# One Strassen-type quarter more in every second column block of a SwiGLU gate/up product

## The chip, the cores and the metric

The kernel runs on one core of one Trainium2 chip. The metric is the device time of one execution in microseconds. Before the change three runs gave 1871.19, 1870.19 and 1870.70 us; the median is 1870.7 us.

## The reference

One layer of a streaming encoder, 256 tokens of width 2048 in float32: a half-step SwiGLU feed-forward, a mixer with a state-space part and an attention part, a second half-step SwiGLU feed-forward, and a gated per-layer embedding. The change is in the second feed-forward:

```python
def swiglu(h, w_gate, w_up, w_down):
    return (jax.nn.silu(h @ w_gate) * (h @ w_up)) @ w_down
...
        x = x + 0.5 * swiglu(rms_norm(x, ffn2_norm[i]), ffn2_w_gate[i], ffn2_w_up[i], ffn2_w_down[i])
```

Here h is 256 x 2048, w_gate and w_up are 2048 x 5632, w_down is 5632 x 2048.

## The kernel before

**Tiles.** P is 128 and NB is 512. The 256 tokens are two token tiles (TT = 2), the inner dimension of 2048 is sixteen k tiles of 128 (KD = 16), handled four at a time (a quarter of the inner dimension, four quarters in all), and the 5632 columns are eleven column blocks of 512 (NF = 11), numbered f = 0 to 10. A weight quarter of one matrix, 512 x 512 values or 1 MB, comes by one DMA on the SP queue into a tile `raw`, of which there are three. It is used in two halves of two k tiles each.

**Precision.** Every float32 product is made from three products of a rounded format. `split` (L165 to L171) makes a high part (`whi`) by a cast on ScalarE (ACT, L168) and a low part (`wlo`) by a subtraction on VectorE (DVE, L171), both 128 x 1024 for one half. There are four buffers for `whi` and for `wlo`. The activations are split the same way (`nhi`/`nlo`, or `hhi`/`hlo` for the first two quarters of the second feed-forward). A matmul is 128 x 128 by 128 x 512. One half, for both token tiles, takes 12 of them (`gemm_half`, L292, L293 and L297), so a weight quarter takes 24, and a quarter of gate and up together 48.

**The seven products.** In the second feed-forward, blocks f = 1 to 10 treat the first quarter of gate and up in another way (`gemm_seven`). The activations of that quarter are a 2 x 2 matrix of blocks (two token tiles by two halves), the weights are one too (two halves by gate and up: b11 and b21 the halves of gate, b12 and b22 those of up). The 2 x 2 product is made with seven block products instead of eight, in Winograd's form of Strassen's method. Each block product is six matmuls (L452, L453, L455), so the quarter takes 42 instead of 48. Three of the products (P1, P2, P3) use b11, b21 and b22 as they are. The four others (P4 to P7) use sums of weight blocks t1 = b11 + b12, t2 = t1 + b22, t4 = t2 + b21 and t3 = b12 + b22, made on DVE at L459 (tile `sum`, two buffers) and split into `shi`/`slo` (three buffers). The sums of activation blocks that go with them are made once, in f = 0, by `sum_forms`, and kept.

Written order of the products: P1, P2, P5, P6, P4, P7, P3. After that come the other three quarters of gate (12 matmuls to a half, onto the PSUM banks of P2 and P4), then those of up (onto the banks of P3 and one more, the tile p38). `opened` (L531 to L533) reads P1, P6 and P7 out of PSUM after the seven products, `gated` (L537 to L540) reads P2, P4 and P5 after the gate quarters and applies the SiLU, and L545 and L547 close the block. A transpose on DVE (L203, `turned`) and 16 small DMAs on the SP queue for every two blocks (L216, `hT<-mid`) lay the result out for the down product.

**Order.** The program text is not the order of execution: the framework's planner reorders the instructions of each engine by its own costs, and then each engine runs its list strictly in order, waiting on semaphores. `put_off(n, fn)` hands work to the n-th following `step()`. PSUM has four single banks (`acc`) and two double ones (`aux`). A block uses all six: P1, P2, P4, P5 in `acc`, P6 with P7 and P3 with its neighbour in `aux`.

**Buffers of activations.** `halves("n")` has four tiles. The second feed-forward's input uses two of them (its quarters 2 and 3), and `sum_forms` a third. `com("h")` has two tiles of 128 x 1024.

Of the kernel before, what the change touches and what calls it, by code (L numbers as in the profile page):

```python
# [9 lines left out]
F32 = mybir.dt.float32  # L10
# [6 lines left out]
P = 128  # L17
# [9 lines left out]
NB = 512  # L27
# [6 lines left out]
def layer_kernel(ctx: ExitStack, tc: tile.TileContext, a: dict, shapes: dict, out: bass.AP):  # L34
# [29 lines left out]
    def uid(s):  # L64
        count[0] += 1
        return f"{s}_{count[0]}"
# [98 lines left out]
    def split(hi, lo, src, scale=None, pinned=False):  # L165

        if scale is None:
            copy = nc.scalar.copy(hi, src)  # L168
            if pinned:
                pin(copy)  # L170
            nc.vector.tensor_tensor(out=lo, in0=src, in1=hi.bitcast(F32), op=ALU.subtract)  # L171
        else:
            split_each(hi.unsqueeze(1), lo.unsqueeze(1), src.unsqueeze(1), [scale])
# [104 lines left out]
    def weight_halves(w, k0, nk, n0, own=None):  # L278

        raw = wp.tile([P, 4, NB], F32, tag="raw", name=uid("raw"), bufs=3)  # L280
        src = w[k0 * P : (k0 + nk) * P, n0 : n0 + NB].rearrange("(j p) n -> p j n", p=P)
        nc.sync.dma_start(raw[:, :nk, :], src)
        return weight_split(raw, nk, own)
# [141 lines left out]
        split(*both, sums.rearrange("p (z t) -> p z t", z=4))  # L425
        return both

    def gemm_seven(act, sums, ws, n0, nkt, pool, first, second):

        raws = []  # L430
        for w in ws:
            raw = wp.tile([P, 4, NB], F32, tag="raw", name=uid("raw"), bufs=3)
            nc.sync.dma_start(raw, w[: 4 * P, n0 : n0 + NB].rearrange("(j p) n -> p j n", p=P))
            raws.append(raw)
        b11, b21, b12, b22 = (raw[:, 2 * h : 2 * h + 2, :] for raw in raws for h in range(2))
        parts = act(0)

        def whole(k, t):
            return [[u[:, 2 * k + j, t * P : (t + 1) * P] for j in range(2)] for u in parts]

        def summed(z):
            return [[u[:, z, j * P : (j + 1) * P] for j in range(2)] for u in sums]

        def product(ps, left, src, own, stop):
            hi, lo = (
                (pool if own else wp).tile([P, 2, NB], F32R, tag=s, name=uid(s), bufs=3 if own else None)
                for s in (("shi", "slo") if own else ("whi", "wlo"))
            )
            split(hi, lo, src)
            lh, ll = left  # L450
            for j in range(2):
                nc.tensor.matmul(ps, lhsT=lh[j], rhs=hi[:, j], start=j == 0, stop=False)  # L452
                nc.tensor.matmul(ps, lhsT=ll[j], rhs=hi[:, j], start=False, stop=False)  # L453
            for j in range(2):
                nc.tensor.matmul(ps, lhsT=lh[j], rhs=lo[:, j], start=False, stop=stop and j == 1)  # L455

        def add(x, y):
            t = pool.tile([P, 2, NB], F32, tag="sum", name=uid("sum"), bufs=2)
            nc.vector.tensor_tensor(out=t, in0=x, in1=y, op=ALU.add)  # L459
            return t  # L460

        p1, p2 = acc(), acc()
        product(p1, whole(0, 0), b11, False, True)
        product(p2, whole(1, 0), b21, False, False)
        step()
        t1 = add(b11, b12)
        p5 = acc()
        product(p5, summed(0), t1, True, True)
        t2 = add(t1, b22)
        p67 = aux()  # L470
        product(p67[:, :NB], summed(1), t2, True, True)
        step()
        t4 = add(t2, b21)
        p4 = acc()
        product(p4, whole(1, 1), t4, True, False)
        t3 = add(b12, b22)
        product(p67[:, NB:], summed(2), t3, True, True)
        step()
        p38 = aux()
        product(p38[:, :NB], summed(3), b22, False, False)  # L480
        step()
        put_off(0, first, p1, p67)
        for w, banks, fresh in ((ws[0], [p2, p4], False), (ws[1], [p38[:, :NB], p38[:, NB:]], True)):
            for k0 in range(4, nkt, 4):
                part = act(k0 // 4)
                for half in list(weight_halves(w, k0, 4, n0)):
                    begin = k0 == 4 and half[0] == 0
                    end = k0 + 4 >= nkt and half[0] == 1
# [3 lines left out]
            if not fresh:  # L492
                put_off(0, second, p2, p4, p5)
        return p38

    def ffn(i, xn, nxt, bg=None):
        wg, wu, wd = (a[f"ffn{i}_w_{s}"][0] for s in ("gate", "up", "down"))
# [22 lines left out]
        for f in range(NF):  # L520
            if prep and f == min(early, NF - 1):
                finish(prep)
                side.close()
                prep = None
                hp = pools.enter_context(phase(f"h{i}b"))
            if sevens and f:
                sg, hh = com("sg"), com("h")
                gate_cols, up_cols = ([u[:, t * NB : (t + 1) * NB] for t in range(TT)] for u in (sg, hh))

                def opened(p1, p67, g=gate_cols, u=up_cols):  # L530
                    nc.scalar.copy(g[0], p1)  # L531
                    nc.vector.tensor_tensor(out=u[0], in0=p67[:, :NB], in1=g[0], op=ALU.add)
                    nc.vector.tensor_tensor(out=u[1], in0=p67[:, NB:], in1=u[0], op=ALU.add)  # L533

                def gated(p2, p4, p5, g=gate_cols, u=up_cols, hh=hh):
                    for z, (ps, other) in enumerate(((p2, g[0]), (p4, u[1]))):
# [3 lines left out]
                    nc.vector.tensor_tensor(  # L540
                        out=v, in0=p5.unsqueeze(1).to_broadcast([P, TT, NB]), in1=v, op=ALU.subtract
                    )

                p38 = gemm_seven(xn, sums, (wg, wu), f * NB, KD, sevens, opened, gated)
                nc.vector.tensor_tensor(out=hh, in0=p38, in1=hh, op=ALU.add)  # L545
                for t in range(TT):
                    nc.vector.scalar_tensor_tensor(  # L547
                        out=up_cols[t], in0=up_cols[t], scalar=xn.rs(t), in1=gate_cols[t], op0=ALU.mult, op1=ALU.mult
                    )
# [1001 lines left out]
```

## Time and profile before

| | before |
|---|---|
| median of three runs | 1870.7 us (1870.19 to 1871.19) |
| the profiled execution, its own time | 1872.24 us |
| its span, first to last instruction | 1870.4 us |
| TensorE (PE) busy | 1859.4 us, 9134 matmuls |
| VectorE (DVE) busy | 1310.4 us, 70% |
| ScalarE (ACT) busy | 996.5 us, 53% |
| granted TensorE clock | 1.0 throughout |

PE is the matrix engine and PEld its weight loads, which overlap the matmuls; SPq is the queue that issues DMAs. A line of a timeline has the start, the duration, the engine, the source line, the operation and its tiles, and in brackets how long the engine was idle before and what ended the wait. The seven-product blocks f = 1 to 10 lie between 1097.5 and 1523.3 us of the span; "block" below means one f.

### The profile page before, as it was taken

What the parts mean: (1) busy time and instruction counts of PE and PEld (TensorE: products, weight loads), DVE (VectorE), ACT (ScalarE), POOL (GpSimd) and SP (SyncE); (2) the same over time, 40 slices, a digit from 0 to 9 for tenths busy, and PEclk for the clock granted to TensorE, in tenths of its full rate; (3) what the DMA queues carried; (4) which work ended last, traced back from release to release, by engine and by line L of the source; (5) the groups of instructions that cost most, each with busy time, mean ns of one, the idle gap of its engine ahead of it and who ended that gap; (6) DMA issues with size and microseconds to landing.
All of it is one profiled execution on the core that took longest, in us unless ns stands there. A gap on an engine that the chain in (4) does not pass through costs nothing.

```text
span 1870.4 us, 23938 instructions
## 1 busy us (share of the span) xinstructions
PE 1859.4 (99%) x9134; PEld 1536.3 (82%) x9134; DVE 1310.4 (70%) x1527; ACT 996.5 (53%) x1151; POOL 50.4 (3%) x84
## 2 busy tenths in 40 slices
PE   9999999999999999999999999999999999999998
PEld 7888888888888888878888888888888888888887
DVE  8867665455576776687567678778787866777655
ACT  7444444444456665456695555445454555666554
POOL 0011000000000000010020000000000000000000
PEclk9999999999999999999999999999999999999999
DMA  8788867766655666675645666575666675656563
GB/s 323 242 278 268 267 208 222 231 217 200 217 196 199 212 199 244 185 248 163 222 147 189 218 205 221 203 220 186 203 205 208 225 228 203 204 202 212 189 224 124
DMA packets 230387, 400.06 MB, mean 214 GB/s; under 512 B 26401, under 2 KB 50337, under 8 KB 229985
## 3 DMA queue, kind: packets, MB, share of 16 engines
q1 hardware_dynamic: 227824, 392.81, 63.7%
q0 software_dynamic: 1728, 4.33, 0.7%
q8 instruction: 71, 1.16, 0.3%
q10 hardware_dynamic: 720, 1.41, 0.2%
q14 instruction: 44, 0.35, 0.1%
HBM read 369.26 MB, written 9.83 MB: 203 GB/s over the span
## 4 chain that ended last, share of the span: by engine, by line
PE 92%; ACT 3%; DVE 2%; DMA 1%; SPq 1%; issue 1%; POOL 0%; DVEq 0%; ACTq 0%; POOLq 0%
PE acc L292 26%; PE acc L297 26%; PE acc L293 26%; PE aux L293 3%; PE aux L292 3%; PE aux L297 3%; ACT whi L168 1%; SPq L1061 1%; PE acc L455 1%; DMA raw<-in_w_in 1%; PE aux L452 1%; PE acc L452 1%; PE acc L453 1%; PE aux L455 1%; PE aux L453 1%
## 5 line engine op out<-in xcount | busy, mean ns | idle before, releaser
L171 DVE TENSOR_TENSOR wlo<-raw,whi 128x1024 fp32r<-128x1024 f32 x656 | 798.2, 1224 | 458.9 <-ACT whi L168 455.3
L168 ACT CAST whi<-raw 128x1024 fp32r<-128x1024 f32 x656 | 686.2, 1053 | 758.7 <-PE acc L293 607.9
L292 PE MATMUL acc<-whi,nhi 128*128 128x512 f32 x1408 | 551.0, 391 | 1.2 <-ACT whi L260 0.5
L293 PE MATMUL acc<-whi,nlo 128*128 128x512 f32 x1408 | 548.2, 389 | 0.0
L297 PE MATMUL acc<-wlo,nhi 128*128 128x512 f32 x1408 | 384.4, 389 | 0.0
L292 PE MATMUL acc<-whi,hhi 128*128 128x512 f32 x816 | 317.6, 389 | 0.0
L293 PE MATMUL acc<-whi,hlo 128*128 128x512 f32 x816 | 317.5, 389 | 0.0
L292 PEld LDWEIGHTS acc<-whi,nhi 128*128 128x128 f32 x1408 | 264.3, 188 | 58.3 <-ACT whi L168 1.7
L297 PEld LDWEIGHTS acc<-wlo,nhi 128*128 128x128 f32 x1408 | 264.2, 188 | 55.6 <-DVE wlo L171 0.4
L293 PEld LDWEIGHTS acc<-whi,nlo 128*128 128x128 f32 x1408 | 264.4, 188 | 54.0
L297 PE MATMUL acc<-wlo,hhi 128*128 128x512 f32 x816 | 221.0, 389 | 0.0
L297 PEld LDWEIGHTS acc<-wlo,hhi 128*128 128x128 f32 x816 | 152.8, 188 | 32.5 <-DVE wlo L171 0.9
L293 PEld LDWEIGHTS acc<-whi,hlo 128*128 128x128 f32 x816 | 153.2, 188 | 32.0
L292 PEld LDWEIGHTS acc<-whi,hhi 128*128 128x128 f32 x816 | 153.1, 188 | 31.8
L171 DVE TENSOR_TENSOR hlo<-hT,hhi 128x1024 fp32r<-128x1024 f32 x88 | 107.1, 1218 | 0.0
L168 ACT CAST hhi<-hT 128x1024 fp32r<-128x1024 f32 x88 | 91.8, 1044 | 0.5 <-PE acc L455 0.4
L292 PE MATMUL aux<-whi,nhi 128*128 128x512 f32 x160 | 62.2, 389 | 0.0
L293 PE MATMUL aux<-whi,nlo 128*128 128x512 f32 x160 | 62.2, 389 | 0.0
L297 PE MATMUL aux<-wlo,nhi 128*128 128x512 f32 x160 | 49.3, 389 | 0.0
L171 DVE TENSOR_TENSOR slo<-sum,shi 128x1024 fp32r<-128x1024 f32 x40 | 48.6, 1214 | 0.4 <-ACT shi L168 0.2
L168 ACT CAST shi<-sum 128x1024 fp32r<-128x1024 f32 x40 | 42.1, 1052 | 11.5 <-DVE sum L459 11.4
L297 PEld LDWEIGHTS aux<-wlo,nhi 128*128 128x128 f32 x160 | 30.0, 188 | 6.2
(312 smaller groups left out, 1314.5 us busy)
## 6 DMA issues: line engine op xcount, KB each, us to landing
raw<-in_ffn_w_up SPq DMA_DIRECT2D x88, 1024.0 KB, 5.9
raw<-in_ffn_w_down SPq DMA_DIRECT2D x88, 1024.0 KB, 5.0
raw<-in_ffn_w_gate SPq DMA_DIRECT2D x86, 1024.0 KB, 5.4
raw<-in_w_in SPq DMA_DIRECT2D x32, 1024.0 KB, 5.5
raw<-in_w_out SPq DMA_DIRECT2D x16, 1024.0 KB, 5.1
raw<-in_w_ple_gate SPq DMA_DIRECT2D x16, 1024.0 KB, 5.1
hT<-mid SPq DMA_DIRECT2D x160, 64.0 KB, 5.0
h<-mid SPq DMA_DIRECT2D x176, 32.0 KB, 3.4
```

The lines of the kernel that those rows point to most:

```text
L168: copy = nc.scalar.copy(hi, src)
L171: nc.vector.tensor_tensor(out=lo, in0=src, in1=hi.bitcast(F32), op=ALU.subtract)
L292: nc.tensor.matmul(ps[t], lhsT=lh, rhs=hi[:, j, cols], start=start and j == 0, stop=False)
L293: nc.tensor.matmul(ps[t], lhsT=ll, rhs=hi[:, j, cols], start=False, stop=False)
L297: nc.tensor.matmul(ps[t], lhsT=lh, rhs=lo[:, j, cols], start=False, stop=stop and j == 1)
L452: nc.tensor.matmul(ps, lhsT=lh[j], rhs=hi[:, j], start=j == 0, stop=False)
L453: nc.tensor.matmul(ps, lhsT=ll[j], rhs=hi[:, j], start=False, stop=False)
L455: nc.tensor.matmul(ps, lhsT=lh[j], rhs=lo[:, j], start=False, stop=stop and j == 1)
L1061: nc.sync.dma_start(zt[0][p1 : p1 + HC, z], sv[p0 : p0 + HC, r % 2 * 2 + r // 2])
```

## The change

`gemm_seven` becomes a class `Seven` with the same seven products, and blocks with odd f (1, 3, 5, 7, 9) take two quarters through them, the second between the gate quarters and the up quarters: seven products of quarter 0, gate quarters 2 and 3, seven products of quarter 1, up quarters 2 and 3. The banks of the seven products go on accumulating over both. Blocks with even f still take one quarter. In odd blocks `opened` and `gated` both come after the second seven products; in even blocks they stay after the first seven products and after the gate quarters. The written order of the products is now P1, P5, P6, P4, P7, P2, P3, everywhere. `sum_forms` runs for quarters 0 and 1.

```diff
+    class Seven:
...
+        def product(self, z, left, src, own):
             hi, lo = (
-                (pool if own else wp).tile([P, 2, NB], F32R, tag=s, name=uid(s), bufs=3 if own else None)
+                (self.pool if own else wp).tile([P, 2, NB], F32R, tag=s, name=uid(s), bufs=3 if own else None)
                 for s in (("shi", "slo") if own else ("whi", "wlo"))
             )
             split(hi, lo, src)
+            ps = self.bank(z)
+            begin = self.done == 0
+            end = self.done == self.chunks - 1 and z in ((1, 5, 6, 7, 2, 4) if self.closing else (1, 5, 6, 7))
...
+        def chunk(self, kb):
+
+            raws = []
+            for w, n0 in self.ws:
+                raw = wp.tile([P, 4, NB], F32, tag="raw", name=uid("raw"), bufs=3)
+                nc.sync.dma_start(
+                    raw, w[4 * kb * P : 4 * (kb + 1) * P, n0 : n0 + NB].rearrange("(j p) n -> p j n", p=P)
+                )
+                raws.append(raw)
+            b11, b21, b12, b22 = (raw[:, 2 * h : 2 * h + 2, :] for raw in raws for h in range(2))
+            parts, sums = self.act(kb), self.sums(kb)
...
+            self.product(1, whole(0, 0), b11, False)
+            t1 = self.add(b11, b12)
+            self.product(5, summed(0), t1, True)
+            step()
+            t2 = self.add(t1, b22)
+            self.product(6, summed(1), t2, True)
+            t4 = self.add(t2, b21)
+            self.product(4, whole(1, 1), t4, True)
+            step()
+            t3 = self.add(b12, b22)
+            self.product(7, summed(2), t3, True)
+            self.product(2, whole(1, 0), b21, False)
+            step()
+            self.product(3, summed(3), b22, False)
+            step()
+            self.done += 1
+
+        def column(self, side, kbs):
+
+            banks = [self.bank(z) for z in ((2, 4), (3, 8))[side]]
+            w, n0 = self.ws[side]
+            for kb in kbs:
+                part = self.act(kb)
+                for half in list(weight_halves(w, 4 * kb, 4, n0)):
+                    end = kb == self.last and half[0] == 1 and not (side == 0 and self.closing)
                     for t in range(TT):
-                        gemm_half({t: banks[t]}, (part, half), (t,), fresh and t == 1 and begin, end)
+                        begin = (side, t) == (1, 1) and kb == self.chunks and half[0] == 0
+                        gemm_half({t: banks[t]}, (part, half), (t,), begin, end)
                     step()
...
+                chunks = 1 + f % 2
+                s = Seven(xn, lambda kb: sums[kb], ((wg, f * NB), (wu, f * NB)), KD, sevens, chunks, chunks == 2)
+                rest = range(chunks, KD // 4)
+                s.chunk(0)
+                if chunks == 1:
+                    put_off(0, opened, s)
+                s.column(0, rest)
+                if chunks == 2:
+                    s.chunk(1)
+                    put_off(0, opened, s)
+                put_off(0, gated, s)
+                s.column(1, rest)
...
-                sums = sum_forms(xn(0))
+                sums = [sum_forms(xn(kb)) for kb in range(2)]
```

More of the change, by code (lines that the diff above doesn't have):

```diff
@@ L426, in sum_forms, with __init__, bank @@
         return both
[L428 to L444, printed above, removed]
+    class Seven:
+        def __init__(self, act, sums, ws, nkt, pool, chunks, closing=False):
+            self.closing = closing
+            self.act, self.sums, self.ws, self.pool = act, sums, ws, pool
+            self.chunks, self.last = chunks, nkt // 4 - 1
+            self.banks = {}
+            self.done = 0
+        def bank(self, z):
+            if z not in self.banks:
+                if z in (1, 2, 4, 5):
+                    self.banks[z] = acc()
+                else:
+                    double = aux()
+                    for i, zz in enumerate((6, 7) if z in (6, 7) else (3, 8)):
+                        self.banks[zz] = double[:, i * NB : (i + 1) * NB]
+                    self.banks[6.7 if z in (6, 7) else 3.8] = double
+            return self.banks[z]
+        def product(self, z, left, src, own):
             hi, lo = (
-                (pool if own else wp).tile([P, 2, NB], F32R, tag=s, name=uid(s), bufs=3 if own else None)
+                (self.pool if own else wp).tile([P, 2, NB], F32R, tag=s, name=uid(s), bufs=3 if own else None)
                 for s in (("shi", "slo") if own else ("whi", "wlo"))
@@ L454, in product, with add @@
             for j in range(2):
-                nc.tensor.matmul(ps, lhsT=lh[j], rhs=lo[:, j], start=False, stop=stop and j == 1)
-        def add(x, y):
-            t = pool.tile([P, 2, NB], F32, tag="sum", name=uid("sum"), bufs=2)
+                nc.tensor.matmul(ps, lhsT=lh[j], rhs=lo[:, j], start=False, stop=end and j == 1)
+        def add(self, x, y):
+            t = self.pool.tile([P, 2, NB], F32, tag="sum", name=uid("sum"), bufs=2)
             nc.vector.tensor_tensor(out=t, in0=x, in1=y, op=ALU.add)
@@ L477, in gemm_seven, with whole, summed @@
[L477 to L488, printed above, removed]
+        def chunk(self, kb):
[8 more added lines that the diff above has]
+            parts, sums = self.act(kb), self.sums(kb)
+            def whole(k, t):
+                return [[u[:, 2 * k + j, t * P : (t + 1) * P] for j in range(2)] for u in parts]
+            def summed(z):
+                return [[u[:, z, j * P : (j + 1) * P] for j in range(2)] for u in sums]
+            self.product(1, whole(0, 0), b11, False)
[14 more added lines that the diff above has]
+            self.done += 1
@@ L540, in gated @@
                     nc.vector.tensor_tensor(
[L541 removed]
+                        out=v, in0=s.bank(5).unsqueeze(1).to_broadcast([P, TT, NB]), in1=v, op=ALU.subtract
                     )
[L544 to L545 removed]
+                chunks = 1 + f % 2
[10 more added lines that the diff above has]
+                s.column(1, rest)
+                nc.vector.tensor_tensor(out=hh, in0=s.banks[3.8], in1=hh, op=ALU.add)
                 for t in range(TT):
```

32 lines of the change are left out of this document (7 added, 25 removed).

## The prediction, made before the changed kernel was run

> **What bounds the kernel now.** The page comes first: span, busy times, and the chain of waits that ended last.
>
> ```profile
> span 1870.4 us, 23938 instructions
> PE 1859.4 (99%) x9134; PEld 1536.3 (82%) x9134; DVE 1310.4 (70%) x1527; ACT 996.5 (53%) x1151; POOL 50.4 (3%) x84
> PE 92%; ACT 3%; DVE 2%; DMA 1%; SPq 1%; issue 1%; POOL 0%; DVEq 0%; ACTq 0%; POOLq 0%
> ```
>
> TensorE sets the end, so a matmul removed is time saved as long as its operands arrive. For this stage the view by stretches follows, cut at the first matmul of each block f = 1 to 10; columns are length, then busy us and count of PE, weight loads, DVE, ACT, POOL, then granted clock, DMA share, GB/s.
>
> ```profile
> 1097.50:1139.79 42.29, 42.29 (x187) 34.91 (x186) 32.91 (x33) 21.16 (x23) 0.00 (x0) 1.00 0.59 199
> 1139.79:1182.26 42.47, 42.47 (x187) 34.83 (x186) 31.14 (x31) 20.55 (x22) 0.00 (x0) 1.00 0.71 223
> 1182.26:1225.14 42.88, 42.74 (x187) 34.68 (x186) 37.31 (x37) 22.09 (x24) 0.00 (x0) 1.00 0.57 196
> 1225.14:1267.49 42.35, 42.35 (x187) 34.83 (x186) 31.15 (x31) 20.56 (x22) 0.00 (x0) 1.00 0.72 224
> 1267.49:1310.42 42.93, 42.79 (x187) 34.68 (x186) 37.30 (x37) 22.10 (x24) 0.00 (x0) 1.00 0.57 196
> 1310.42:1352.79 42.37, 42.37 (x187) 34.83 (x186) 31.15 (x31) 20.57 (x22) 0.00 (x0) 1.00 0.72 224
> ...
> 1438.07:1480.95 42.88, 42.73 (x187) 34.68 (x186) 37.22 (x37) 22.09 (x24) 0.00 (x0) 1.00 0.57 196
> 1480.95:1523.29 42.34, 42.34 (x187) 34.79 (x186) 31.34 (x31) 20.98 (x23) 0.00 (x0) 1.00 0.76 239
> sum 425.79, PE 425.22 PEld 347.72 DVE 337.88 ACT 212.79 POOL 0.00; mean PE 42.52 PEld 34.77 DVE 33.79 ACT 21.28 POOL 0.00
> ```
>
> A block has 186 matmuls (42 + 144). What they cost undisturbed is read from the timeline of PE over 96 of them, eight halves:
>
> ```profile
> 1160.51 0.39 PE L292 MATMUL acc<-whi,nhi 128*128 128x512 f32 x1
> ...
> 1182.26 0.39 PE L452 MATMUL acc<-whi,hhi 128*128 128x512 f32 x1
> ```
>
> (1182.26 - 1160.51) / 96 = 0.2266 us, so a block needs 42.14. The ten lose 425.79 - 421.4 = 4.4 us, 0.44 on average; even f lose about 0.22, odd f from 3 on about 0.77. Where, the timeline of DVE at f = 3 shows, beside two rows of f = 2:
>
> ```profile
> 1130.94 1.22 DVE L459 TENSOR_TENSOR sum<-raw,raw 128x1024 f32<-128x1024 f32 x1
> 1132.19 1.22 DVE L459 TENSOR_TENSOR sum<-sum,raw 128x1024 f32<-128x1024 f32 x1
> ...
> 1139.01 1.22 DVE L171 TENSOR_TENSOR wlo<-raw,whi 128x1024 fp32r<-128x1024 f32 x1
> ...
> 1178.80 1.22 DVE L459 TENSOR_TENSOR sum<-raw,raw 128x1024 f32<-128x1024 f32 x1
> 1180.05 1.23 DVE L459 TENSOR_TENSOR sum<-sum,raw 128x1024 f32<-128x1024 f32 x1
> ...
> 1183.61 1.22 DVE L545 TENSOR_TENSOR h<-aux,h 128x1024 f32<-128x1024 f32 x1
> 1184.74 1.22 DVE L171 TENSOR_TENSOR slo<-sum,shi 128x1024 fp32r<-128x1024 f32 x1
> 1185.87 1.41 DVE L547 SCALAR_TENSOR_TENSOR h<-h,sm,sg 128x512 f32<-128x512 f32 x2
> 1187.20 1.22 DVE L459 TENSOR_TENSOR sum<-sum,raw 128x1024 f32<-128x1024 f32 x1
> 1188.33 0.71 DVE L203 STREAM_TRANSPOSE mid<-h 128x512 f32<-128x512 f32 x1
> ...
> 1192.93 2.35 DVE L171 TENSOR_TENSOR wlo<-raw,whi 128x1024 fp32r<-128x1024 f32 x2
> 1195.19 0.69 DVE L532 TENSOR_TENSOR h<-aux,sg 128x512 f32<-128x512 f32 x1
> ```
>
> From 1132.19 to 1139.01 stand six operations of 1024 columns start to start: 1.137 us each. At f = 2 the sums begin 8.85 us before PE (1139.79), at f = 3 only 3.46 (1182.26), and there the tail of the block before (L545, twice L547, two transposes, about 3.7 us by these starts) stands between them. The waits name what PE then lacks:
>
> ```profile
> PEld aux L452 <- ACT shi L168: 2.7, 5, 0.6
> PEld acc L452 <- ACT shi L168: 0.9, 4, 0.2
> ```
>
> The reader is to see that the seven products are the one place here where DVE is nearly too slow: 11 operations (seven low parts, four sums), 12.5 us, for 42 matmuls, 9.52 us. It lives on the 32.6 us of plain quarters after them.
>
> **The change part by part.** All differences are on the span, and what lies around it (1872.24 - 1870.4 us in this execution) stays. This execution lies 1.5 us above the median of the runs, 1870.7; the sum is put on that median.
>
> *Matmuls.* Five blocks lose six each: 30 x 0.2266 = **-6.80 us**.
>
> [...]
>
> *The work that replaces them.* Each of the five new sevens has 11 DVE operations where the plain quarter had four: seven more, 8.0 us, and three more casts of about a microsecond on ACT, which is busy 22 of 42.88. It is hidden behind PE only as far as DVE runs ahead: an odd block's 37.3 busy become 45.3 in about 41.5, and the even one's 31.15 of 42.35 must lend the difference. Without that cover all 8.0 would show. I price a new seven as the old ones: 0.44 on average, five times **+2.2 us**, bounds 0.14 (f = 1) and 0.79 (f = 5), that is +0.7 and +4.0.
>
> *The second seven begins early enough, barely.* There are three raw buffers and a seven holds two. The DMA issues:
>
> ```profile
> 1173.52 0.37 SPq L282 DMA_DIRECT2D raw<-in_ffn_w_gate  x1
> 1188.48 2.10 SPq L282 DMA_DIRECT2D raw<-in_ffn_w_gate  x2
> 1195.35 6.23 SPq L282 DMA_DIRECT2D raw<-in_ffn_w_up  x3
> SPq L282 <- DVE sum L459: 130.6, 19, 14.5
> raw<-in_ffn_w_up SPq DMA_DIRECT2D x39, 1024.0 KB, 5.9
> ```
>
> The quarter fetched at 1173.52 sits in the third buffer; its splits are the pair at 1192.93, and at 1195.35 the buffer is free again. In the changed block that issue is the second seven's up quarter: it lands 5.9 us later, at 1201.3. PE ends the first seven at 1225.14 - 144 x 0.2266 = 1192.5 and 48 matmuls later, at 1203.4, wants it. Lead 2.1 us. From landing, nine DVE operations (10.2 us) and a last pair of low-part matmuls (0.45) remain, against 9.52 of PE: 1.1 us of lead are enough, so it holds by a microsecond. Behind SP's waits stand the other weight quarters, and in even blocks the small hT DMAs; the number of deferred steps in a block stays 16, so these stay in the even blocks.
>
> *Even blocks.* They now follow a seven at 10.9 us instead of 32.6. Their lead falls from 8.85 us to two or three. The loss goes from 0.22 towards the odd blocks' 0.77: 0 to +2.75 in five; middle, **+1.4 us**.
>
> *Order of products, `opened` moved.* P2 and P3 need no sum; both now come last, so where PE waits for `shi` the planner can pull two products (2.7 us) forward instead of one, and in odd blocks L532 and L533 leave the first seven. If this mends the odd blocks' excess of 0.55, four times: -2.2. Against it, the gate raw was last read by t4 (1187.20) and is now last read by P2's split, up to three operations (3.4 us) later: the issue at 1188.48 would be at 1191.9, landing at 5.9 more, 1197.8, and with a cast of one microsecond PE, due there at 1192.5 + 24 x 0.2266 = 1197.9, would wait 0.9. I price the outer bound at a third of that, as splits of another quarter can go first: 15 x 0.3 = +4.5. Of a gain of 2.2 and nothing, which the rows show, I take the middle: **-1.1 us**.
>
> *Second `sum_forms`.* One whole sum, four short ones, one split at f = 0:
>
> ```profile
> 1075.40 0.76 DVE L423 TENSOR_TENSOR h<-h 128x256 f32<-128x256 f32 x2
> 1076.08 0.88 DVE L423 TENSOR_TENSOR h<-h,h 128x256 f32<-128x256 f32 x2
> 1079.14 1.22 DVE L171 TENSOR_TENSOR nlo<-h,nhi 128x1024 fp32r<-128x1024 f32 x1
> 1084.29 1.23 DVE L171 TENSOR_TENSOR wlo<-raw,whi 128x1024 fp32r<-128x1024 f32 x1 [1.44 <-ACT whi L168]
> 1087.01 1.23 DVE L171 TENSOR_TENSOR wlo<-raw,whi 128x1024 fp32r<-128x1024 f32 x1 [1.50 <-ACT whi L168]
> ```
>
> About 1.2 + 1.6 + 1.2 = 4.0 us of DVE once; the gaps behind it cover 2.9, the early start before f = 1 the rest: 0, at worst +4.0. It takes the fourth of four `n` tiles, needed next by the block after this feed-forward, when two are long read. PSUM banks change hands 10.9 us before the next block wants them: 0.
>
> Sum: -6.80 + 2.2 + 1.4 - 1.1 + 0 = **-4.3 us**, so 1870.7 - 4.3 = **1866.4 us**. Its own ends: -6.8 + 0.7 + 0 - 2.2 = -8.3 (1862.4) and, with the terms at their upper ends but the outer bound and `sum_forms`, -6.8 + 4.0 + 2.75 + 0 = -0.05 (1870.7).
>
> **The rivals.** *DVE becomes the bound over a pair.* From an odd block's t1 to the end of the next even seven DVE has 9 + 4 + 11 + 4 + 11 = 39 operations (44.3 us), two tails (7.4) and `opened` with `gated` (about 3.6): 55.3. PE has 3 x 9.52 + 96 x 0.2266 = 50.3. With 3.46 us of lead and 0.45 at the end DVE is 2.0 late per pair, where a pair now loses 0.99: five times 1.0 gives -6.8 + 5.0, **1868.9 us**, no change to be told. For it: there is nearly no slack in that stretch; against: it holds at f = 1 less, where the sums have no late start, and tails can be put off.
>
> *The up quarter comes late in even blocks.* `opened` and `gated` (3.6 us) now come right after the second seven; if the planner puts them ahead of the splits that free the third buffer, the lead of 2.1 becomes -1.5. Each us of lead short of 1.1 costs one, so 2.6 in five blocks, without what they lose now (0.22): 5 x 2.4 = 12; with the second sevens at +2.2: -6.8 + 2.2 + 12 = +7.4, **1878.1 us**. It decides from 1.0 us of delay on. For it: SP's waits on L459 show how often the ring of three is the limit; against: the planner put L532 behind the pair at 1192.93.
>
> *The gain is eaten in neither place:* the low end above, 1862.4.
>
> *The change doesn't do what it says:* if the planner left 48 matmuls in a quarter; the text gives 42, so no chance is kept for it.
>
> **How the numbers follow.** This kernel's measurement tells 0.2% (3.7 us) from no change. The forecast's case 0.44, DVE-bound 0.28, late quarter 0.28. The forecast's case reaches into "same" at its upper end, and the DVE-bound case can be a little better than 1867.0, so: faster 0.42, same 0.30, slower 0.28. The likeliest case alone spans 1862.4 to 1870.7; the range takes in the other two: 1862.4 to 1878.1.
>
> **What would show it.** 30 matmuls fewer; odd blocks near 41.3 us (180 x 0.2266 = 40.8 and half a microsecond), even ones 42.4 to 42.9. Right: DVE about 45 busy in odd blocks, PE waiting in tenths. Wrong: PE waiting over a microsecond for `shi` or `slo` at an even block's t4 (DVE-bound), or for a sum behind a raw DMA (late quarter), or any odd block over 42.9.

## The result: slower by 1.15%, and the profile after

Four runs of the changed kernel gave a median of 1891.99 us (1890.32 to 1893.96), against 1870.47 us for the kernel before beside it: ratio 1.0115, interval 1.0097 to 1.0132. That is 21.5 us more, where 4.3 less were forecast. The profiled execution took 1891.26 us.

The page of the changed kernel, in the same order as before:

```profile
span 1889.5 us, 23927 instructions
PE 1862.9 (99%) x9104; PEld 1537.4 (81%) x9104; DVE 1351.1 (72%) x1568; ACT 1012.3 (54%) x1167; POOL 50.3 (3%) x84
PE 93%; DVE 3%; ACT 3%; issue 1%; DMA 0%; POOL 0%; SPq 0%; DVEq 0%; ACTq 0%; POOLq 0%
```

The 30 matmuls are gone (9134 to 9104), yet PE is busy 3.5 us longer: some of the remaining ones took longer. The chain of waits still says PE 93%. It would not lead anyone to the cause. The view by stretches does, cut at the first matmul of each block, columns as in the prediction:

```profile
1095.63:1138.20 42.57, 41.60 (x181) 33.63 (x180) 39.32 (x39) 23.93 (x26) 0.00 (x0) 1.00 0.57 198
1138.20:1180.54 42.34, 42.34 (x187) 34.91 (x186) 32.05 (x32) 20.58 (x22) 0.00 (x0) 1.00 0.72 224
1180.54:1227.85 47.31, 44.35 (x181) 35.64 (x180) 42.57 (x41) 25.14 (x27) 0.00 (x0) 0.93 0.51 178
1227.85:1271.45 43.60, 42.63 (x187) 34.81 (x186) 33.41 (x33) 20.58 (x23) 0.00 (x0) 1.00 0.68 218
1271.45:1317.67 46.22, 43.26 (x182) 34.77 (x180) 42.52 (x41) 25.09 (x27) 0.00 (x0) 0.96 0.52 182
...
sum 446.34, PE 429.65 PEld 348.73 DVE 376.09 ACT 228.16 POOL 0.00; mean PE 42.97 PEld 34.87 DVE 37.61 ACT 22.82 POOL 0.00
```

The ten blocks take 446.34 us instead of 425.79: 20.6 of the 21.5 us lie here. At 0.2266 us a matmul an odd block needs 180 x 0.2266 = 40.79 and an even one 42.14, all ten 414.6; they lose 31.7 us instead of 4.4. The first pair (f = 1, 2) loses 2.0, the pair f = 3 and 4 already 6.5 + 1.5. Two new things stand in the rows of odd f: DVE is busy 42.5 of 46 to 47 us, and the granted clock is under 1. The same view, with the block f = 3 cut before its second seven, and ten microseconds near its start:

```profile
1180.54:1207.30 26.76, 23.80 (x91) 18.74 (x90) 23.23 (x23) 12.38 (x13) 0.00 (x0) 0.87 0.45 157
1207.30:1227.85 20.55, 20.55 (x91) 16.91 (x90) 19.34 (x20) 12.76 (x15) 0.00 (x0) 1.00 0.58 204
1180.00:1190.00 10.00, 7.04 (x24) 5.08 (x23) 9.26 (x10) 4.21 (x4) 0.00 (x0) 0.78 0.15 39
```

Each half of the block has 90 matmuls, 20.39 us. The half with the second seven, on which the forecast had spent its care, loses 0.16. The first seven loses 6.37: 26.76 - 23.80 = 2.96 of PE idle, and 23.80 - 20.39 = 3.41 of matmuls that run slower. The timeline of PE shows both, and the wait of the even block after it:

```profile
1181.90 0.40 PE L460 MATMUL acc<-shi,nhi 128*128 128x512 f32 x1
...
1183.15 0.73 PE L463 MATMUL acc<-slo,nhi 128*128 128x512 f32 x2 [0.15 <-DVE slo L171]
1186.69 0.80 PE L460 MATMUL aux<-shi,nhi 128*128 128x512 f32 x1 [2.81 <-ACT shi L168]
...
1187.71 0.63 PE L460 MATMUL aux<-shi,nhi 128*128 128x512 f32 x1
1188.14 0.63 PE L461 MATMUL aux<-shi,nlo 128*128 128x512 f32 x1
...
1192.67 0.39 PE L460 MATMUL acc<-whi,hhi 128*128 128x512 f32 x1
...
1234.04 0.50 PE L460 MATMUL acc<-shi,hhi 128*128 128x512 f32 x1 [0.97 <-ACT shi L168]
```

P1 and P5 run, then P6 (`aux<-shi`, the first of the double bank) waits 2.81 us for its cast; after that matmuls start 0.43 us apart (1187.71 to 1188.14) instead of 0.2266, until about 1192.5, so for almost six microseconds. P2 (1192.67), which needs no sum, stands behind all of it. The sum that P6 waits for is t2, and the timeline of DVE says where it was; the last row is t1 of the second seven:

```profile
1177.08 1.22 DVE L467 TENSOR_TENSOR sum<-raw,raw 128x1024 f32<-128x1024 f32 x1
1178.66 1.23 DVE L171 TENSOR_TENSOR wlo<-raw,whi 128x1024 fp32r<-128x1024 f32 x1 [0.36 <-ACT whi L168]
1180.74 1.22 DVE L578 TENSOR_TENSOR h<-aux,h 128x1024 f32<-128x1024 f32 x1 [0.86 <-PE aux L297]
1181.88 1.22 DVE L171 TENSOR_TENSOR slo<-sum,shi 128x1024 fp32r<-128x1024 f32 x1
1183.02 1.41 DVE L580 SCALAR_TENSOR_TENSOR h<-h,sm,sg 128x512 f32<-128x512 f32 x2
1184.34 1.22 DVE L467 TENSOR_TENSOR sum<-sum,raw 128x1024 f32<-128x1024 f32 x1
...
1201.16 1.22 DVE L467 TENSOR_TENSOR sum<-raw,raw 128x1024 f32<-128x1024 f32 x1
```

t1 begins 3.46 us before PE's first matmul, as before the change. Then come a split and the tail of the block before (L578, L580); L578 itself waits 0.86 us for PE to finish that block, so DVE is not behind with its work here: its list holds it. t2 begins at 1184.34, 7.3 us after t1. In the kernel before, t2 followed t1 at once and only then came the tail. The second seven's t1 stands 6.1 us ahead of PE (1207.30). The waits of PE over the whole stage repeat the picture:

```profile
PE aux L460 <- ACT shi L168: 11.2, 4, 2.8
PE acc L460 <- ACT shi L168: 3.9, 4, 1.0
```

Four waits of 2.8 at P6 (odd f from 3 on) and four of 1.0 at P4 (even f from 4 on). They sum to 15 us; about as much again is lost in slower matmuls and small gaps.

### The profile page after: what moved, and what is told of

Read it like the earlier page. It is cut to its first block, busy times and chain, and to the rows that moved or that the text cites. A ratio compares the mean times of both kernels' runs of the same rounds, so it can differ in the third digit from the quotient of the medians.

```text
span 1889.5 us, 23927 instructions
## 1 busy us (share of the span) xinstructions
PE 1862.9 (99%) x9104; PEld 1537.4 (81%) x9104; DVE 1351.1 (72%) x1568; ACT 1012.3 (54%) x1167; POOL 50.3 (3%) x84
## 4 chain that ended last, share of the span: by engine, by line
PE 93%; DVE 3%; ACT 3%; issue 1%; DMA 0%; POOL 0%; SPq 0%; DVEq 0%; ACTq 0%; POOLq 0%
PE acc L292 26%; PE acc L297 26%; PE acc L293 26%; PE aux L293 2%; PE aux L292 2%; PE aux L297 2%; PE acc L460 1%; PE aux L460 1%; PE acc L461 1%; PE aux L463 1%; PE aux L461 1%; PE acc L463 1%; ACT shi L168 1%; DVE slo L171 1%; ACT whi L168 1%; DVE h L580 1%
## 5 line engine op out<-in xcount | busy, mean ns | idle before, releaser
L293 PE MATMUL acc<-whi,hlo 128*128 128x512 f32 x776 | 302.3, 390 | 0.0
L292 PE MATMUL acc<-whi,hhi 128*128 128x512 f32 x776 | 302.2, 389 | 0.0
L297 PE MATMUL acc<-wlo,hhi 128*128 128x512 f32 x776 | 209.1, 389 | 0.0
L297 PEld LDWEIGHTS acc<-wlo,hhi 128*128 128x128 f32 x776 | 145.7, 188 | 30.3
L292 PEld LDWEIGHTS acc<-whi,hhi 128*128 128x128 f32 x776 | 145.6, 188 | 30.4
L293 PEld LDWEIGHTS acc<-whi,hlo 128*128 128x128 f32 x776 | 145.7, 188 | 30.1
L168 ACT CAST shi<-sum 128x1024 fp32r<-128x1024 f32 x60 | 62.6, 1049 | 42.2 <-DVE sum L467 42.2
L171 DVE TENSOR_TENSOR slo<-sum,shi 128x1024 fp32r<-128x1024 f32 x60 | 72.6, 1212 | 2.0 <-ACT shi L168 2.0
L460 PE MATMUL aux<-shi,nhi 128*128 128x512 f32 x60 | 25.8, 429 | 11.2 <-ACT shi L168 11.2
```

The lines of the kernel that those rows point to most:

```text
L292: nc.tensor.matmul(ps[t], lhsT=lh, rhs=hi[:, j, cols], start=start and j == 0, stop=False)
L293: nc.tensor.matmul(ps[t], lhsT=ll, rhs=hi[:, j, cols], start=False, stop=False)
L297: nc.tensor.matmul(ps[t], lhsT=lh, rhs=lo[:, j, cols], start=False, stop=stop and j == 1)
L460: nc.tensor.matmul(ps, lhsT=lh[j], rhs=hi[:, j], start=begin and j == 0, stop=False)
```

## The experiments

Two explanations were set against each other. By *place* (A in the expectations), the fault is that the tail of the block before has come to stand ahead of t2 in DVE's list, where the new order of products wants t2 early. By *supply* (C), the order of the list matters little: three sevens with only 10.9 us of plain work between them ask more of DVE than it can give there, and PE waits wherever that shows. Ratios, and the microseconds better or worse, are against the kernel before, measured beside each; the changed kernel stands at +21.5 us.

**The old order of products, the rest of the change kept.**

```diff
             self.product(1, whole(0, 0), b11, False)
+            self.product(2, whole(1, 0), b21, False)
+            step()
             t1 = self.add(b11, b12)
             self.product(5, summed(0), t1, True)
-            step()
             t2 = self.add(t1, b22)
...
-            self.product(2, whole(1, 0), b21, False)
```

> Two quarters in odd blocks as in the changed kernel, the products in the order of before (P1, P2, P5, P6, P4, P7, P3). Theory A, the place of t2 in DVE's list: the second quarter makes the planner put the tail of the block before (the closing sum and two products) ahead of t2, whatever the order; P2 gives PE 1.36 us more to do before P6, so the wait of 2.8 us at P6 in odd blocks falls to about 1.4 and is too short for the clock to drop: odd blocks near 44 us instead of 46.2 to 47.4, and 1872 to 1882 in all. Theory B, the new written order alone does it: the wait is gone, odd blocks near 41.3, 1864 to 1868.

1884.19 us beside 1872.14, ratio 1.0064 (1.0049 to 1.0079): +12.0 us. Its blocks f = 3 and 4, and the stretch from t1 of f = 3 to the last low part of the seven of f = 4, in the view by stretches:

```profile
1180.05:1223.41 43.36, 41.98 (x182) 33.42 (x181) 41.21 (x40) 23.32 (x25) 0.00 (x0) 1.00 0.57 194
1223.41:1268.24 44.83, 42.94 (x188) 34.75 (x186) 33.55 (x33) 22.34 (x24) 0.00 (x0) 1.00 0.67 212
1176.58:1237.96 61.38, 58.11 (x250) 46.01 (x249) 57.90 (x57) 33.63 (x35) 0.00 (x0) 1.00 0.49 165
```

The clock stays at 1.00, with waits of PE at P6 of 0.95 us at f = 3 and 1.44 at f = 4, and the pair still loses (43.36 - 40.79) + (44.83 - 42.14) = 5.3 us. Through three sevens DVE is busy 57.90 of 61.38 us, that is 94%: little is left in it to be used better. The written order explains a part; the larger part is there without it. The time lies above both ranges of the expectation. The run does not part place from supply, for in its list, too, the tail stands ahead of t2 at f = 3 (L578 at 1180.25, t2 at 1183.85).

**The new order alone**, one quarter in every block, as before the change.

```diff
-                chunks = 1 + f % 2
+                chunks = 1
...
-                sums = [sum_forms(xn(kb)) for kb in range(2)]
+                sums = [sum_forms(xn(kb)) for kb in range(1)]
```

> One quarter in every block as before the change, the products in the new order; the second set of activation sums is left out, as nothing uses it. Theory A: no wait near 2.8 us, t2 stands ahead of the tail, 1869 to 1874. Theory B: the odd blocks wait 2.8 us and then run at a lower clock, four times 5 to 6 us, 1888 to 1896.

1878.79 us beside 1872.14, ratio 1.0032 (1.0019 to 1.0045): 6.7 us worse than before (3.6 to 8.4 by the interval), between the two ranges of the expectation. In its list t2 does stand ahead of the tail. PE has one wait in each odd block from f = 3 on, at P4, for t4's cast. First P4 of f = 3 in the kernel before (its first matmul there is at 1182.26), then, from the timeline of the new order alone, f = 3 and f = 7:

```profile
1189.60 0.46 PE L452 MATMUL acc<-shi,hhi 128*128 128x512 f32 x1
```

```profile
1181.05 0.39 PE L460 MATMUL acc<-whi,hhi 128*128 128x512 f32 x1
...
1188.53 0.50 PE L460 MATMUL acc<-shi,hhi 128*128 128x512 f32 x1 [1.48 <-ACT shi L168]
...
1361.89 0.50 PE L460 MATMUL acc<-shi,hhi 128*128 128x512 f32 x1 [1.48 <-ACT shi L168]
```

Before, P4 started 7.34 us after the first matmul: P1, P2, P5, P6, P3 and two matmuls of a plain quarter stood ahead of it. Now P2 comes last, PE is ready for P4 after 1188.53 - 1.48 - 1181.05 = 6.0 us, and waits about what it gained, one product of 6 x 0.2266 = 1.36 us. P2 had been the cover of the late sums. The two waits are equal, but not what follows. The view by stretches, blocks f = 3 and 7 and five microseconds around each wait:

```profile
1181.05:1225.46 44.41, 42.88 (x187) 34.73 (x186) 37.49 (x37) 23.42 (x25) 0.00 (x0) 1.00 0.57 189
1354.41:1400.40 45.99, 44.46 (x187) 35.93 (x186) 37.58 (x37) 23.42 (x25) 0.00 (x0) 0.96 0.58 183
1187.00:1192.00 5.00, 3.52 (x16) 2.83 (x16) 5.00 (x7) 2.10 (x2) 0.00 (x0) 1.00 0.68 208
1360.00:1365.00 5.00, 3.52 (x10) 2.51 (x9) 5.00 (x6) 2.09 (x2) 0.00 (x0) 0.73 0.60 194
```

In the same 3.52 us of PE, 16 matmuls ran in one and 10 in the other. One wait of 1.48 us costs its block 2.27 us or 3.85.

**t2 written right behind t1**, the rest as in the changed kernel.

```diff
             t1 = self.add(b11, b12)
+            t2 = self.add(t1, b22)
             self.product(5, summed(0), t1, True)
             step()
-            t2 = self.add(t1, b22)
             self.product(6, summed(1), t2, True)
```

> The changed kernel with the sum t2 written directly behind t1, so that it ranks ahead of the split of t1. Theory A: in DVE's list t2 moves ahead of the two closing products and the split, about 2.5 us earlier; the wait at P6 falls from 2.8 to a few tenths and with it the low clock: 1868 to 1876. If t2's place is not the cause, nothing changes: 1889 to 1894.

1884.42 us beside 1872.14, ratio 1.0066 (1.0049 to 1.0082): +12.3 us. The wait of 2.8 us and the low clock are gone (the profile's mean clock is 1.000, in the changed kernel 0.994); its waits of PE over the stage are now

```profile
PE acc L460 <- ACT shi L168: 10.7, 8, 1.5
PE aux L460 <- ACT shi L168: 4.9, 4, 1.2
```

15.6 us in twelve waits where the changed kernel had 15.1 in eight. Waiting has not become less; it has been broken up. Neither range of the expectation was met. In DVE's list t2 moved less than was meant: at f = 3 it passed the split and the two closing products, but still follows the closing sum (L578 at 1180.48, t2 at 1181.62). What came back, 21.5 - 12.3 = 9.2 us, is of the size of what the low clock had cost: 3.41 us at f = 3 and, reckoned in the same way, 11.5 in the four odd blocks from f = 3 on.

**The tail handed to the second step of the next block**, meant to set t2 ahead of it.

```diff
-                nc.vector.tensor_tensor(out=hh, in0=s.banks[3.8], in1=hh, op=ALU.add)
...
-                put_off(2, turned, hp, f, hh)
+                def closed(s, f=f, hh=hh, g=gate_cols, u=up_cols):
+                    nc.vector.tensor_tensor(out=hh, in0=s.banks[3.8], in1=hh, op=ALU.add)
...
+                put_off(1, closed, s)
```

> The changed kernel with the tail of a block (closing sum, two products) handed to the second step of the next block, so that it ranks behind t1, t2 and t4. Theory A: t2 stands ahead of the tail, P6 doesn't wait, the clock stays up, and the 30 matmuls saved show: 1862 to 1868. A rival, DVE as such is too slow over an odd and the next even block: the wait only moves, to t4 or to the even block, 1875 or more.

1887.67 us beside 1872.14, ratio 1.0081 (1.0066 to 1.0096): +15.5 us, as the rival in the expectation had it. The edit did what was meant only at f = 3 and in the even blocks. At f = 5, 7 and 9 the closing sum (L582) stays ahead of t2, which begins at 1269.16 at f = 5, and DVE stands idle until PE has finished the block:

```profile
1266.88 1.23 DVE L582 TENSOR_TENSOR h<-aux,h 128x1024 f32<-128x1024 f32 x1 [2.44 <-PE aux L297]
```

There PE still waits 1.48 us at P6. At f = 3, where t2 is early, P6 does not wait and P4 waits 0.46; in the even blocks, with t2 early but t4 behind the closing sum, PE waits 1.0 to 1.4 us at P4. So the early t2 mends the wait at P6 and not those at P4, and the run does not decide between *place* and *supply*.

**Without the low parts of the weight sums:** the 60 subtractions that make `slo` are left out, and their matmuls read the high part again. PE's work is the same, DVE's less by 60 operations.

```diff
-            split(hi, lo, src)
...
+                nc.scalar.copy(hi, src)
+                lo = hi
```

> The changed kernel without the low parts of the four weight sums: the subtraction on DVE is left out and the matmuls of the low phase read the high part instead, so the number of matmuls and their order in the text stay. A seven then has 7 DVE operations instead of 11. Theory C, DVE can't supply an odd block's two sevens and the next even block's in time: with 4.5 us less of DVE per seven the waits for shi vanish, odd blocks near 41 and even ones near 42.3 us, 1862 to 1867. Theory D, the place in the list or late weights hold PE, not the amount of DVE work: waits of a microsecond and more stay, 1875 to 1892.

1861.81 us beside 1871.99, ratio 0.9948 (0.9933 to 0.9962): -10.2 us. From 1090 to 1510 us PE does not stop:

```profile
1090.00:1510.00 420.00, 420.00 (x1847) 346.45 (x1846) 317.50 (x307) 235.34 (x241) 0.00 (x0) 1.00 0.67 215
```

Some 30 us come back for 60 operations off DVE. The time is that of *supply*, a fifth of a microsecond under its range. But the list of DVE came out differently here too (all four sums ahead of the closing sum), and no matmul waits for `slo` any more, so *place* is mended along with it. The spread version below keeps both the operations and their results.

**t4 and t3 on POOL**, which is nearly idle: with two quarters and the old order, with one quarter, and with the later tail.

```diff
-            t4 = self.add(t2, b21)
+            t4 = self.add(t2, b21, nc.gpsimd)
...
-            t3 = self.add(b12, b22)
+            t3 = self.add(b12, b22, nc.gpsimd)
```

> Two quarters in odd blocks, products in the order of before, and the sums t4 and t3 made on POOL, which is idle here, instead of DVE; all results stay. DVE has 9 operations per seven instead of 11. Theory C: of the 5.3 us lost per pair of blocks without this, three times 2.3 us of DVE go, and the loss falls below 2 per pair: 1866 to 1872. Theory D: no better than 1882 to 1886. If POOL is much slower than DVE at this sum (over 3 us), P4 and P7 wait for it and it is worse.

> One quarter in every block and the products in the order of before, so the kernel before, with t4 and t3 on POOL; the second set of activation sums is left out, as nothing uses it. Theory C: the odd blocks lose 0.2 instead of 0.77 us, 1867 to 1870. If POOL's sums disturb DVE or come late, 1872 to 1880.

> As the run with the sums on POOL and two quarters in odd blocks, and the tail of a block (closing sum, two products) handed to the second step of the next block. Theory C: as that run or up to 3 us better, 1863 to 1871, as both the amount and the place are mended. Theory D: the tail later made no gain before and makes none here, 1882 or more.

Slower in all three, and far above the ranges given, but for the open one of the third (1882 or more): 1916.49 us, ratio 1.0232 (1.0215 to 1.0249); 1902.13, 1.0163 (1.0147 to 1.0178); 1914.89, 1.0232 (1.0216 to 1.0247). What came true are conditions named beforehand: a sum of over 3 us on POOL, and a disturbed DVE. Groups of the first, with minimum, median and maximum of one in ns:

```profile
L467 POOL TENSOR_TENSOR sum<-sum,raw x15: 3257/3306/3324, 1093.5 to 1522.4; 128x1024 f32<-128x1024 f32 x15
L171 DVE TENSOR_TENSOR slo<-sum,shi x59: 1171/1220/3422, 1094.4 to 1532.3; 128x1024 fp32r<-128x1024 f32 x59
```

The sum t4 takes 3.3 us on POOL instead of 1.22, and a DVE subtraction takes up to 3.42 instead of 1.22. In the same trace the subtractions that overlap no sum on POOL, 150 of 197 in this stage, all take 1.17 to 1.23 us. The closing sum of a block (L578), which reads one of its inputs from PSUM, keeps to 1.21 to 1.23 us although all nine of them overlap POOL. So in this trace every subtraction of over 1.23 us ran beside a sum on POOL, and had both inputs in SBUF. No run varies the place of the inputs alone, so whether it matters is not shown, and these runs say nothing for or against *supply*.

**The same work, spread.** Two quarters in odd blocks as in the change, the old order of products, and plain quarters between: odd blocks run gate quarter 2, a seven, gate quarter 3, up quarter 2, the other seven, up quarter 3; even blocks three gate quarters, the seven, three up quarters. No seven follows the end of a block any more, and sevens lie 10.9, 21.8 and 21.8 us of plain work apart instead of 10.9, 10.9 and 32.6. The start and stop marks of the banks are counted by product to allow it.

```diff
-                s.chunk(0)
-                if chunks == 1:
-                    put_off(0, opened, s)
-                s.column(0, rest)
                 if chunks == 2:
+                    s.column(0, [2])
+                    s.chunk(0)
+                    s.column(0, [3])
+                    s.column(1, [2])
                     s.chunk(1)
                     put_off(0, opened, s)
-                put_off(0, gated, s)
-                s.column(1, rest)
+                    put_off(0, gated, s)
+                    s.column(1, [3])
+                else:
+                    s.column(0, [1, 2, 3])
+                    s.chunk(0)
+                    put_off(0, opened, s)
+                    put_off(0, gated, s)
+                    s.column(1, [1, 2, 3])
```

> Two quarters in odd blocks, products in the order of before, all the work kept, but the sevens apart from the tail and from each other: an odd block runs gate quarter 2, the first seven, gate quarter 3, up quarter 2, the second seven, up quarter 3; an even block runs its three gate quarters first, then the seven, then up. Theory C in its form of a bunch: over a pair of blocks DVE is busy about 76 of 82 us, so it can supply both if the sevens don't meet the tail; waits of PE under 0.5 us, odd blocks 41.0, even ones 42.3, 1862 to 1867. Rival: DVE's total is too near PE's, or the planner's list puts other work in front, and waits of a microsecond stay: 1870 to 1885.

1863.82 us (1863.32 to 1864.53) beside 1871.78, ratio 0.9954 (0.9939 to 0.9969): -8.0 us, in the range of theory C and the best version that computes everything. Its page has the counts of the changed kernel on PE, DVE and ACT:

```profile
PE 1852.2 (99%) x9104; PEld 1532.1 (82%) x9104; DVE 1348.8 (72%) x1568; ACT 1012.8 (54%) x1167; POOL 50.3 (3%) x84
```

The view by stretches over the stage, and its one wait of PE:

```profile
1090.00:1510.00 420.00, 419.55 (x1840) 344.30 (x1839) 378.71 (x367) 234.20 (x241) 0.00 (x0) 1.00 0.67 214
```

```profile
PE aux L470 <- ACT shi L168: 0.4, 1, 0.4
```

DVE is busy 90% of these 420 us, and PE waits 0.4. The timelines of DVE and PE at the first seven of f = 3 show the lead:

```profile
1176.14 1.22 DVE L477 TENSOR_TENSOR sum<-raw,raw 128x1024 f32<-128x1024 f32 x1
...
1178.86 1.22 DVE L477 TENSOR_TENSOR sum<-sum,raw 128x1024 f32<-128x1024 f32 x1
1180.00 1.22 DVE L594 TENSOR_TENSOR h<-aux,h 128x1024 f32<-128x1024 f32 x1
...
1187.05 1.22 DVE L477 TENSOR_TENSOR sum<-sum,raw 128x1024 f32<-128x1024 f32 x1
...
1185.05 0.39 PE L470 MATMUL acc<-whi,hhi 128*128 128x512 f32 x1
```

t1 begins 8.9 us before PE wants the seven, instead of 3.46; a plain quarter (5.4 us) stands between the end of the block before and the seven. The tail (L594 and what follows it) has not gone from between the sums, but t2 stands ahead of it, t4 behind it still begins only 2.0 us after PE's first matmul of the seven, and PE has the plain quarter to run meanwhile. So neither the amount of work nor the order within a seven was the cause by itself, but that amount in that place.

**The controls to it:** spread with the new order of products, spread with one quarter in every block, spread with two in every block.

```diff
-                chunks = 1 + f % 2
+                chunks = 1
```

```diff
-                chunks = 1 + f % 2
+                chunks = 2
```

> As the run with two quarters spread apart in odd blocks, but with the products in the new order of the changed kernel. Theory C: with the tail out of the sevens' way the order is worth little, 1862 to 1867. If the new order by itself makes PE wait at P4, as it did in the run with one quarter (1.48 us in odd blocks), 1867 to 1875.

> One quarter in every block, with the three gate quarters first, then the seven, then up, so that no seven meets the tail; the second set of activation sums is left out, as nothing uses it. Theory C: the odd blocks' loss of 0.77 us goes, 3 us in all, 1867 to 1869. If the loss has to do with the seven itself, it stays at 1870 to 1872.

> All ten blocks with two quarters through the seven products, spread in each as in the spread odd blocks. DVE then has 30 operations of 1.137 us, the tail, opened and gated per block, about 41.4 us, and PE 180 x 0.2266 = 40.8. Theory C: DVE is the bound in every block, waits of PE come back all along, blocks of 42 us and more; 60 matmuls fewer give 13.6 us at most, I expect 1862 to 1885. If the amount of DVE work were not the cause, 1857 to 1860.

The new order, spread: 1864.91 us, ratio 0.9962 (0.9948 to 0.9976). This is the changed kernel with nothing but the sevens moved, and it is the run that shows the cause: with the same operations, their place makes the difference between +21.5 and -6.3 us. The order that cost 6.7 us without cover costs one or two here, and the two intervals overlap, so even that is not clear. Two things were moved at once, though: a seven no longer follows the end of a block, and the sevens stand more evenly apart. No run with this amount of work moves one without the other.

One quarter, spread: 1867.61 us, ratio 0.9976 (0.9966 to 0.9986), with no wait of PE in the stage. So of the 8 us about 4 come from mending the old losses and 3.8 from the second quarter. The 30 matmuls are worth 6.8; where the other 3.0 go was only followed so far: in the same 420 us of the stage the records hold 1840 matmuls with the second quarter and 1850 without it (10 x 0.2266 = 2.3 us), and only 0.4 of that is a wait that the profile lists.

Two quarters in every block, spread: 1890.04 us, ratio 1.0095 (1.0078 to 1.0112). Over the same 420 us:

```profile
1090.00:1510.00 420.00, 401.22 (x1700) 319.97 (x1699) 390.11 (x374) 227.07 (x236) 0.00 (x0) 0.98 0.59 196
```

DVE at 93%, PE standing still for 19 us: here spreading helps no more. The time is above the range expected. By the expectation's own sum every block now has 41.4 us of DVE for 40.8 of PE, and sevens stand 10.9 us apart throughout, so here the amount of work is enough to hold PE back.

## Why the prediction was wrong

*Matmuls, -6.80: right.* 30 fewer, and the kernels that keep DVE ahead of PE show part (spread: 3.8 us more than with one quarter) or most (no low parts: -10.2 against -4.2 for one quarter spread) of their worth.

*The second seven begins early enough, barely: right.* The step took the issue of its up quarter at 1195.35 in the old trace, 13.09 us after the block's first matmul. The DMA queue of the changed kernel has it 13.09 us after 1180.54:

```profile
1193.63 0.37 SPq L475 DMA_DIRECT2D raw<-in_ffn_w_up  x1
```

It landed at 1199.65. The seven's t1 then stood 6.1 us ahead of PE, and its half of the block lost 0.16 us. But the microsecond of margin was not put to the test: PE came 6.37 us late. Without that it would have wanted the seven at 1180.54 + 20.39 = 1200.93, a lead of 1.3 us where the step needed 1.1 (its 2.1 held 0.7 of the old block's own loss). The rival of a late up quarter did not occur. *Second `sum_forms`, 0: right.* The stage begins at 1095.63, and in the run of the new order alone, which makes one set of sums, at 1095.90.

*Order of products, -1.1: wrong in sign.* Alone it costs 6.7 us. The step read the late position of P2 and P3 as a stock from which the planner could pull forward. PE took its list in the order set before the run: at f = 3 P3 (1188.56) came forward, P2 (1192.67) did not, and P2 behind P1 had been 1.36 us of cover that every sum lost. The upper bound of +4.5 was priced from another thing, a late raw buffer, of which nothing is seen.

*The work that replaces them, +2.2, and even blocks, +1.4: mis-sized, and the main failure.* Both took the loss of a seven from the kernel before, as if it belonged to the seven. It depends on where the seven stands and on the lead that DVE has there. Even blocks from f = 4 on lose 1.4 each, not 0.5. The first seven of odd blocks from f = 3 on, which the working gave no new price at all (it was the "old" seven), loses 5.3 to 6.5 instead of 0.77. These four make 23.4 of the 31.7 us. They are not the ones that follow another seven closely: 32.6 us of plain work lie before them, as in the kernel before, and t1 has the same lead of 3.46 us. What is new there is the tail ahead of t2, and P2 no longer ahead of the sums. That distance counts too is seen at f = 1, whose second seven follows the first at 10.9 us:

```profile
1116.15:1138.20 22.05, 21.08 (x91) 16.74 (x90) 21.86 (x23) 12.90 (x15) 0.00 (x0) 1.00 0.55 191
```

The half before it took 20.52 us for its 20.39, so PE was not late, t1 (1111.46) had a lead of 4.7 us, and this half still loses 22.05 - 20.39 = 1.66. The bound of +4.0 was taken from the worst old block, and in the old trace neither a seven 10.9 us behind another nor a tail ahead of t2 occurs.

*The rival "DVE becomes the bound over a pair": the mechanism was right, the price not.* It gave 55.3 us of DVE from t1 of the odd block to the end of the even seven and 2.0 us of lateness. With the old order that stretch took 61.38 us: 57.90 busy, since splits of the quarters behind the sevens stand between (41 operations of 1024 columns in the list, not 39), and 3.5 idle, waiting for casts and for PE. Lateness was then 61.4 - 50.3 - 3.5 = 7.6 us, or 8.0 with the 0.45 at the end, and the pair lost 5.3: fifteen matmuls of plain quarters, 3.4 us, run ahead of the last pair of the seven of f = 4, which the sum had not counted on. In the changed kernel the order and the clock bring it to 8.0. The forecast had five pairs at 2.0; there came one at 2.0 and four at (31.7 - 2.0) / 4 = 7.4.

*The granted clock* was in no term. In the four odd first sevens 11.5 us of the 23.4 are matmuls that take longer, and the granted clock is under 1 in each of these four blocks (0.93, 0.96, 0.93, 0.96); 9.2 us came back with the early t2, at a mean clock of 1.000 and without less waiting (15.6 us for 15.1).

The signs named in advance did their work: odd blocks over 42.9 (46.2 to 47.4), and PE waiting for `shi`, though at t2 of odd blocks more than at t4 of even ones. DVE was 42.5 busy in odd blocks from f = 3 on, not 45, as part of its work ran on into the even ones (33.4 at f = 4 against 31.15 before). What stays open is how much of the loss is the tail ahead of t2 and how much the distance between sevens, and why the planner set the tail there, which its costs would tell and no run here tried.

## What to carry to other kernels

A helper engine's average share says little about whether it holds the main engine back: the same 1568 DVE operations gave 1892 us bunched and 1864 us spread, at 72% on both pages. Before work is moved from the bounding engine to a helper, count what the helper must deliver from the end of one demand to the end of the next, compare it with the time there (here 90% busy over the stage held PE up by 0.4 us, 93% by 19), and give the helper a lead before each demanding stage: here both an even spacing and a plain stage after the end of a block did this, and they were not tried apart. An operation that needs nothing late, like P2, was worth about its own length as cover where it stood (1.36 us), so it isn't free to move.

## What was not expected of the hardware

The granted clock fell after waits of PE much shorter than a block of 42 us, and not after every one of the same length. With 2.81 us of waiting it was 0.78 over ten microseconds (1180 to 1190), with matmuls 0.43 us apart after the wait. In the run of the new order alone it was 0.73 in the five microseconds around the wait of 1.48 us at f = 7 (10 matmuls in 3.52 busy us) and 1.00 in those around the same wait at f = 3 (16). In the run with t2 early, with twelve waits of 1.2 to 1.5 us, the profile's mean stayed 1.000. The trace of the new order alone has the low clock of f = 7:

```profile
1362.28:1365.69 3.41, 3.41 (x10) 2.67 (x9) 3.41 (x5) 1.05 (x1) 0.00 (x0) 0.50 0.99 323
```

The clock is at half for 3.41 us from 1362.28, that is 0.39 us after the wait of f = 7 ended (1360.41 to 1361.89). At f = 9, where a wait of 1.47 us ended at 1450.16, matmuls start 0.43 us apart again, from 1451.34 to 1453.48. After the waits of 1.48 us at f = 3 (1187.05 to 1188.53) and f = 5 (1273.73 to 1275.21) all matmuls but the first started 0.23 us apart. What parts the two waits that slow matmuls followed from the two others, these runs do not show.

With POOL as a helper DVE's own subtractions took up to 2.8 times as long (3.42 us against 1.22), all of the slowed ones beside a sum on POOL, so an idle engine was not a free one.
